# Two sums made by accumulating transfers from GpSimd's queue, and two more convolution steps in each round

## The chip, the cores and the metric

The kernel runs on one core of one Trainium2 chip. The metric is the device time of one execution in microseconds (us); lower is better. Each kernel is run several times, and medians are compared.

## The reference, cut to what matters

Two layers follow each other on 1024 latent tokens of width 1024. The first, an even layer, has two branches. Branch A gates and convolves over 31 tokens, normalises and gates again. Branch B runs a gated linear recurrence over the tokens in both directions and adds the two. One output projection takes both branches, and the result is added to the tokens `x`:

```python
va, vg, ga, xb, gb = jnp.split(h @ p["w_in"], ...)
y_a = conformer_conv(va, vg, p) * jax.nn.silu(ga)     # u = va*sigmoid(vg); conv; layernorm; silu
hs, hT = lru_scan(a, bx, h0, with_outputs)            # both directions
y_b = hs[:, :, 0] + hs[::-1, :, 1]                    # sum of the two directions
y_b = y_b * jax.nn.silu(gb)
out = jnp.concatenate([y_a, y_b], axis=-1) @ p["w_out"]
x = x + gate * out
```

The second layer, a pooling mixer, is not touched. Everything is fp32.

## The kernel before, in words

**Products.** Channels lie on the 128 partitions in 8 blocks (KT = 8), the 1024 tokens along the free axis in two halves of 512 (HALF, H = 512). An fp32 product is three matmuls on operands that are split into a high and a low part. For each weight of 128x1024, ScalarE casts the high part (`wh`) and GpSimd makes the low part (`wl = wr - wh`), in `raw_split`. PE uses `wl` in every third matmul, so it waits for GpSimd only there.

**The fixed order.** From the rounds to the end of the `ga` products, the helper `on` (line 670, which is why most rows carry L670) puts every instruction of an engine behind the one issued before it on that engine. So ScalarE, VectorE, GpSimd and PE do their work in the order in which the program is written: an instruction that waits holds back all that stand behind it. Transfers on SP's queue are placed by a scheduler.

**The rounds.** A loop over the 8 blocks j (L903) computes on PE `vg`, `va`, the gate matrices of the recurrence and `xb` of the next block. In round j, the recurrence of block j-1 (its state is `st`) goes on beside it: `rec_input` and the wide product on GpSimd, `rec_tanh` and `rec_exp` on ScalarE, and on VectorE `rec_scan`, two scans for each of the two directions. The tiles of a state, 128x1280 each (256 context and 1024 latent tokens), change their roles from round to round, so ScalarE writes a tile in the next round that was scanned in this one. At the round's end `rec_sum` adds the two directions on VectorE (128x1024) and SP stores the sum, 512 KB, to `yb_raw[j]` in DRAM. The residual of the next weight on GpSimd comes right behind. The 31-tap convolution of branch A is cut into steps on VectorE, one tap or pair of taps each. `fill(n)` puts n of these steps where it stands. A round ends with `fill(6)`; what is left of the convolutions is done behind the rounds.

**Behind the rounds.** The products `gb` 1 to 7 follow. `gated(n)` loads `yb_raw[n]` back in two halves (`yr`, L1223), multiplies it with `silu(gb)` (`sb`), splits it into `ybh` and `ybl`, and so forms the operand of the next product. That is `wob`, the second branch's share of the output projection: 8 blocks m of two halves. After each half `wob_evict` (L1254) scales PE's result on ScalarE into a tile `wo`, SP loads the half of the tokens `xT` into `xp`, GpSimd adds `wo` to it, and SP stores it to `x1_part` in DRAM (256 KB each). Much later `woa` (L1528) reads `x1_part` back and adds the first branch's share. Beside blocks 6 and 7 of `wob` runs the layer norm of branch A: squares on ScalarE into tiles `lsq`, sums on VectorE. Behind `wob` come the products `ga` of blocks 0 and 4.

**The ring of ScalarE's tiles.** `wo`, `lsq`, `sq_ln`, `mh`, `ml`, `sb` and others come from one pool, `tpool`, with four buffers (L60). A new tile can be written only when the last reader of the tile four places before it is done.

Of the kernel before, what the change touches and what calls it, by code (L numbers as in the profile page):

```python
# [17 lines left out]
C = 256  # L18
# [4 lines left out]
HALF = (slice(0, H), slice(H, S))  # L23
# [28 lines left out]
def body(ctx, tc, xT, ctxT, cc, ccol, modT, modW, win, gw, wout, wu, grp, wg, wo1, small, edge, ident, outT):  # L52
    nc = tc.nc
    mult, add, sub = ALU.mult, ALU.add, ALU.subtract
# [12 lines left out]
    yb_raw = [dram.tile([P, S], F32, tag=f"yb_raw{j}", name=f"yb_raw{j}") for j in range(KT)]  # L67
    y_raw = [{n: dram.tile([P, 2 * S], F32, tag=f"y_{n}_{p}", name=f"y_{n}_{p}") for n in BOPS} for p in range(2)]
    x1_part = [dram.tile([P, S], F32, tag=f"x1_part{j}", name=f"x1_part{j}") for j in range(KT)]
# [7 lines left out]
    def ttile(name):  # L77
        return tpool.tile([P, H], F32, tag="t", name=name)
# [22 lines left out]
    def held(after):  # L101
        return tc.issue_after(after.ins) if after is not None else nullcontext()
# [71 lines left out]
    def col(o, n=1):  # L174
        return sm[:, o : o + n]
# [121 lines left out]
    with ExitStack() as sctx:  # L297
# [36 lines left out]
        def cast(eng, n, part=slice(0, D)):  # L334
            hi = gs[n[1]][0] if isinstance(n, tuple) else w_tiles(n)[0]
            f = eng.copy if eng is A else lambda o, i: eng.tensor_copy(out=o, in_=i)
            f(hi[:, part], raws[n][:, part])
# [295 lines left out]
        for i in range(2):  # L633
            v = cx[i].rearrange("p (k n) -> p k n", n=C)
# [31 lines left out]
    def on(eng, f, *args, **kw):  # L666
        with ExitStack() as octx:
            if eng in last:
                octx.enter_context(tc.issue_after(last[eng].ins))
            last[eng] = f(*args, **kw)  # L670
        return last[eng]

    def act(*args, **kw):
        return on("act", nc.scalar.activation, *args, **kw)
# [4 lines left out]
    def gp(*args, **kw):  # L679
        return on("pool", nc.gpsimd.tensor_tensor, *args, **kw)  # L680
# [11 lines left out]
    def all_of(steps):  # L692
        for _ in steps:
            pass

    def raw_load(src, name):
        raw = wpool.tile([P, D], F32, tag="wr", name=f"wr_{name}")
        nc.sync.dma_start(raw, src)
        return raw
# [21 lines left out]
    def vec(f, **kw):  # L721
        return on("vec", f, **kw) if fixed[0] else f(**kw)
# [78 lines left out]
    def at_rest():  # L801
        ln_sums()
        while spread_[0] < min(whole_[0], ended[0] + 2, NSPREAD):
            spread_sum()
# [4 lines left out]
    def fill(n):  # L809
        while n > 0:  # L810
            try:
                next(going[0])
                n -= 1
            except StopIteration:
                if begun[0] >= whole_[0]:
                    return
                going[0] = conv(begun[0])
                begun[0] += 1

    with ExitStack() as actx:  # L820
# [42 lines left out]
        def rec_scan(st, d):  # L863
            at, iu = st[2][2 * d : 2 * d + 2]
            vec(nc.vector.scalar_tensor_tensor, out=iu, in0=at, scalar=1.0, in1=iu, op0=add, op1=mult)
            if d == 0:
                ctx_, lat = slice(0, C), slice(C, E)
                first = iu[:, C - 1 : C]
            else:
                ctx_, lat = slice(C - 1, None, -1), slice(E - 1, C - 1, -1)  # L870
                first = iu[:, 0:1]
            vec(nc.vector.tensor_tensor_scan, out=iu[:, ctx_], data0=at[:, ctx_], data1=iu[:, ctx_],
                initial=0.0, op0=mult, op1=add)
            vec(nc.vector.tensor_tensor_scan, out=iu[:, lat], data0=at[:, lat], data1=iu[:, lat],
                initial=first, op0=mult, op1=add)

        def rec_sum(st):
            hs, hb = st[2][1], st[2][3]
            vec(nc.vector.tensor_tensor, out=hs[:, C:], in0=hs[:, C:], in1=hb[:, C:], op=add)
            nc.sync.dma_start(yb_raw[st[0]], hs[:, C:])  # L880


        def gate_steps(j, w, u2, gates):
# [18 lines left out]
        state, free = None, [L[0], L[1], L[2], L[3], L[4], L[5]]  # L902
        for j in range(KT):  # L903
            final = j == KT - 1
# [65 lines left out]
            if state is None:  # L970
                for m in range(3 * KT - 2, 3 * KT):
                    gate_dot(m, gate_raw[m - 2 * KT])
                vec(nc.vector.tensor_tensor, out=m0[:, 0, 2 * KT :], in0=m0[:, 0, 2 * KT :],
                    in1=col(O_MB + 2 * KT, KT), op=add)
# [13 lines left out]
            if state is not None:  # L988
                for d in range(2):
                    rec_scan(state, d)  # L990
                rec_sum(state)
            at_rest()
            xb = wide(name if final else f"xb{j + 1}")
            steps = (x for h in range(2) for x in mm3_fixed(xb[:, HALF[h]], wnext, (hh, hl), HALF[h]))
# [12 lines left out]
                    w = raw_split(raw, name)  # L1007
                    rec_input(now, 0)
            all_of(steps)
            fill(19 if state is None else 6)  # L1010
            state, uc = now, ucn


# [38 lines left out]
        gb_product(3, gws[3])  # L1052
        fill(24)
        rec_scan(state, 0)
        raw = raw_load(win[4 * KT + 4], "gb4")
        hi = wpool.tile([P, D], F32R, tag="wh", name="wh_gb4")
        lo = wpool.tile([P, D], F32R, tag="wl", name="wl_gb4")
# [1 line left out]
        vec(nc.vector.tensor_tensor, out=lo, in0=raw, in1=hi.bitcast(F32), op=sub)  # L1059
        gws[4] = hi, lo  # L1060
        rec_scan(state, 1)
        rec_sum(state)
        at_rest()

    cpool.release()
# [4 lines left out]
    def d2tile(name, dt=F32):  # L1070
        return d2pool.tile([P, S], dt, tag="d2", name=name)
# [5 lines left out]
    def vtile(name):  # L1077
        return vpool.tile([P, H], F32, tag="v", name=name)
# [140 lines left out]
    def gated(n, between):  # L1219
        th, tl = d2tile(f"ybh{n}", F32R), d2tile(f"ybl{n}", F32R)  # L1220
        for h in range(2):
            y = vtile(f"yr{n}_{h}")
            nc.sync.dma_start(y, yb_raw[n][:, HALF[h]])  # L1223
            v = sbs[n][h]
            vec(nc.vector.tensor_tensor, out=v, in0=y, in1=v, op=mult)
            cast(th[:, HALF[h]], v)
            gp(out=tl[:, HALF[h]], in0=v, in1=th[:, HALF[h]].bitcast(F32), op=sub)
            fill(between)
        bh.append(th)
        bl.append(tl)  # L1230

    gb_product(4, gws[4])
    gated(0, 3)
    gb_silu(2)
    gb_weights(5)
    gb_product(5, gws[5])
    gated(1, 3)
    for j in range(3, KT + 1):
        if j == 4:
            gb_weights(j + 2)  # L1240
        if j < KT:
            gb_silu(j)
        if 4 < j < KT - 1:
            gb_weights(j + 2)
        if 3 < j < KT - 2:
            gb_product(j + 2, gws[j + 2])
        gated(j - 1, (0, 0, 4, 5, 5, 3, 1, 0)[j - 1])
        if j == KT:
            gb_weights(KT + 1)
            fill(8)  # L1250
        ln_sums()


    def wob_evict(m, h):  # L1254
        v = ttile(f"wo_{m}_{h}")
        act(v, wob_ps[m][h], AF.Identity, scale=m0[:, 0, 2 * KT + m : 2 * KT + m + 1])
        t = vtile(f"xp{m}_{h}")
        nc.sync.dma_start(t, xT[m][:, HALF[h]])
        gp(out=t, in0=t, in1=v, op=add)
        nc.sync.dma_start(x1_part[m][:, HALF[h]], t)  # L1260


    lnmu, lnsq = {}, {}
# [152 lines left out]
    for i in range(KH):  # L1416
        (b11, b12), (b21, b22) = [[us[j][:, h] for h in HALF] for j in (i, KH + i)]
        t1, t2, t3, t4 = b11, ttile(f"yat2_{i}"), b12, b21
        for j in (i, KH + i):
# [4 lines left out]
            for h in range(2):  # L1424
                if i:
# [3 lines left out]
                    v = us[j][:, HALF[h]]  # L1429
# [379 lines left out]
    for m in range(0, NK, 2):  # L1809
# [44 lines left out]
        elif m <= KT:  # L1854
            n = 2 * KT + m - 2
# [203 lines left out]
    def last_half0(m, w, ahead=None, pend=None):  # L2059
        p1, p2, p3, p4, p5, p6, p7 = w  # L2060
        a, d, b = psum(f"qa_l{m}"), psum(f"qd_l{m}"), psum(f"qb_l{m}")
        (x0, x1_), (y0, y1) = [[x1[m + i][:, h] for h in HALF] for i in range(2)]
        with held(linked_[0] if pend is not None else None):
            prod(a, p1, ops["b11"], True, False)
        with tc.high_priority(offset=EVAC):
            evac = nc.scalar.copy(b, a)
        if pend is None:
            mm = prod(d, p4, ops["t4"], True, True)
        else:
            mm = linked(d, p4, ops["t4"], True, True)  # L2070
        with tc.high_priority(offset=EVAC):
            gated(m + 1, y0, d)
        if pend is not None:
            pend("t4")
        nxt = None
        if ahead is not None:
            with tc.issue_after(evac.ins):
                nxt = ahead()
        with tc.issue_after(mm.ins):
            prod(b, p6, ops["t2"], False, False)  # L2080
        with tc.high_priority(offset=EVAC):
            gated(m, x1_, b)
        mm = prod(a, p2, ops["b21"], False, True)
        with tc.high_priority(offset=EVAC):
            gated(m, x0, a)
            fin_add(HALF[0], square(m, HALF[0]))
        with tc.issue_after(mm.ins):
            mm = prod(b, p7, ops["t3"], False, True)
        with tc.high_priority(offset=EVAC):
            gated(m + 1, y0, b)  # L2090
            fin_add(HALF[0], square(m + 1, HALF[0]))
            vec = gated(m + 1, y1, b)
        return nxt, mm, vec

    m = KT - 4
# [7 lines left out]
    wb, _, _ = last_half0(m, wa, last_weights, q2.run)  # L2103
# [230 lines left out]
```

## Time and profile before

| what | value |
|---|---|
| time, median of 3 runs | 1267.25 us (1265.35 to 1271.49) |
| span of the profiled execution | 1263.6 us |
| its own device time | not listed; only the span is |
| TensorE (PE) busy, granted clock | 1249.8 us (99%), 0.998 |
| VectorE (DVE) busy | 1139.3 us (90%) |
| ScalarE (ACT) busy | 653.8 us (52%) |
| GpSimd (POOL) busy | 295.7 us (23%) |

The span runs from the first to the last instruction on the core; the device time has a little around it. A row of the timeline has the start in us, the duration, the engine, the line, the operation with out<-in by the program's names, and in brackets the engine's idle time just before with the instruction or transfer that ended it. A row of the groups has the count, the busy time in us and the mean of one in ns. A row of the DMA issues has the size of one and the median time from issue to landing. A table by stretch has for each engine the busy time in it. The rounds last to about 412 us; the products `gb` to about 500, `wob` to about 586.

### The profile page before, as it was taken

The page shows a single profiled execution, that of the slowest core. Times are in us where ns is not written, and L with a number is a line of the kernel's source. Part 1 is how long each engine was busy: PE and PEld are TensorE (multiplying, and loading weights), DVE is VectorE, ACT ScalarE, POOL GpSimd, SP SyncE. Part 2 cuts the span into 40 slices and gives each one's busy share as a digit, 9 for nine tenths or more (in the row PEclk, how much of TensorE's full clock was granted, in tenths as well). Part 3 has the DMA queues.
Part 4 walks back from the last instruction along what each step waited for, and adds up shares of the span by engine and source line. Part 5 has one row for each costly group of instructions (what it writes and reads, how often), then busy time and mean ns, then how long its engine had stood idle before and what let it go on. Part 6 is the DMA issues. An engine that isn't in the chain of part 4 may idle for free.

```text
span 1263.6 us, 16209 instructions
## 1 busy us (share of the span) xinstructions
PE 1249.8 (99%) x5866; PEld 1035.6 (82%) x5866; DVE 1139.3 (90%) x1746; ACT 653.8 (52%) x952; POOL 295.7 (23%) x176
## 2 busy tenths in 40 slices
PE   9999999999999999999999999999999999999997
PEld 7788888888888888888887878888888888888786
DVE  7799999999999999998978969999899987977975
ACT  8464566656666534237535445744343444644642
POOL 0015364436444547543210023000000000000002
PEclk9999999999999999999999999999999999999999
DMA  9970121112121233442436666344323334759723
GB/s 376 388 254 33 52 65 46 63 43 75 42 84 42 84 119 132 159 150 84 147 112 225 202 206 183 103 136 148 125 94 140 117 125 126 268 199 335 285 71 134
DMA packets 78705, 182.29 MB, mean 144 GB/s; under 512 B 7712, under 2 KB 23328, under 8 KB 78624
## 3 DMA queue, kind: packets, MB, share of 16 engines
q1 hardware_dynamic: 67328, 172.33, 39.8%
q10 hardware_dynamic: 11296, 8.92, 2.2%
q8 instruction: 46, 0.75, 0.2%
q14 instruction: 35, 0.29, 0.1%
HBM read 137.18 MB, written 44.04 MB: 143 GB/s over the span
## 4 chain that ended last, share of the span: by engine, by line
PE 70%; DVE 18%; DMA 7%; issue 2%; ACT 2%; POOL 1%; SPq 0%; POOLq 0%; ACTq 0%; DVEq 0%
PE wob L670 7%; DVE conv L670 5%; PE va L670 5%; PE xb L670 4%; PE vg L670 4%; DVE l L670 3%; PE fold L670 3%; PE g L670 3%; PE qb_v L1153 2%; PE ga L670 2%; PE qb_g L1156 2%; PE ga L161 2%; PE qb_v L1156 2%; PE qb_g L1155 2%; PE qb_g L1153 2%
## 5 line engine op out<-in xcount | busy, mean ns | idle before, releaser
L670 DVE SCALAR_TENSOR_TENSOR conv<-u,sm,conv 128x505 f32<-128x505 f32 (+6 forms) x224 | 153.6, 744 | 1.0
L2045 POOL TENSOR_TENSOR o<-x,rr 128x256 f32<-128x256 f32 (+1 forms) x10 | 9.2, 952 | 448.4 <-ACT rr L2045 448.4
L670 ACT ACTIVATE l<-g,sm 128x512 f32<-128x512 f32 (+1 forms) x96 | 58.7, 619 | 57.7 <-PE g L670 57.0
L670 POOL TENSOR_TENSOR l<-l,l 128x1280 f32<-128x1280 f32 x16 | 47.1, 2967 | 25.6 <-ACT l L670 15.1
L670 PE MATMUL gb<-h0h,wl_gb 128*128 128x512 f32 x128 | 49.9, 390 | 0.4 <-POOL wl_gb L670 0.4
L670 PE MATMUL va<-h0h,wl_va 128*128 128x512 f32 x128 | 49.9, 390 | 0.2 <-DVE wl_va L670 0.2
L98 ACT CAST wq_g<-wr_g 128x512 fp32r<-128x512 f32 x48 | 28.2, 621 | 41.9 <-DMA wr_g<-wg 15.6
L670 PE MATMUL gb<-h0l,wh_gb 128*128 128x512 f32 x128 | 49.8, 389 | 0.0
L670 PE MATMUL gb<-h0h,wh_gb 128*128 128x512 f32 x128 | 49.8, 389 | 0.0
L670 PE MATMUL va<-h0l,wh_va 128*128 128x512 f32 x128 | 49.8, 389 | 0.0
L670 PE MATMUL va<-h0h,wh_va 128*128 128x512 f32 x128 | 49.8, 389 | 0.0
L670 PE MATMUL wob<-ybl,wh_wob 128*128 128x512 f32 x128 | 49.8, 389 | 0.0
L670 PE MATMUL wob<-ybh,wl_wob 128*128 128x512 f32 x128 | 49.8, 389 | 0.0
L670 PE MATMUL wob<-ybh,wh_wob 128*128 128x512 f32 x128 | 49.8, 389 | 0.0
L670 DVE TENSOR_TENSOR_SCAN l<-l,l 128x256 f32<-128x256 f32 (+1 forms) x32 | 48.7, 1521 | 1.1
L670 DVE SCALAR_TENSOR_TENSOR conv<-cL,wsum,conv 128x506 f32<-128x506 f32 (+3 forms) x70 | 48.1, 745 | 0.2
L670 POOL TENSOR_TENSOR l<-l,uc 128x1280 f32<-128x1280 f32 x16 | 47.6, 2999 | 0.0
L98 ACT CAST wq_wo<-wr_wo 128x512 fp32r<-128x512 f32 x48 | 28.6, 620 | 35.5 <-DVE wr_wo L1134 12.4
L98 ACT CAST wq_v<-wr_v 128x512 fp32r<-128x512 f32 x48 | 28.1, 620 | 33.7 <-DMA wr_v<-wfold 16.6
L670 PE MATMUL xb<-h0l,wh_xb 128*128 128x512 f32 x112 | 43.8, 391 | 0.0
L670 PE MATMUL xb<-h0h,wh_xb 128*128 128x512 f32 x112 | 43.8, 391 | 0.0
L670 POOL TENSOR_TENSOR wl_xb<-wr_xb,wh_xb 128x1024 fp32r<-128x1024 f32 x7 | 16.8, 2407 | 114.5 <-ACT wh_xb L670 114.5
(680 smaller groups left out, 4362.5 us busy)
## 6 DMA issues: line engine op xcount, KB each, us to landing
modw<-modW SPq DMA_DIRECT2D x16, 512.0 KB, 10.2
mod<-modT SPq DMA_DIRECT2D x32, 256.0 KB, 3.4
wr_v<-wfold SPq DMA_DIRECT2D x16, 512.0 KB, 4.0
wr_g<-wg SPq DMA_DIRECT2D x16, 512.0 KB, 4.3
wr_wo<-wo SPq DMA_DIRECT2D x16, 512.0 KB, 4.1
mod<-modT SPq DMA_DIRECT2D x14, 512.0 KB, 4.5
y_b<-y SPq DMA_DIRECT2D x24, 256.0 KB, 3.5
y_t<-y SPq DMA_DIRECT2D x24, 256.0 KB, 3.1
```

The lines of the kernel that those rows point to most:

```text
L98: return (nc.scalar.copy(hi, src), eng.tensor_tensor(out=lo, in0=src, in1=hi.bitcast(F32), op=sub))
L161: mm(ps, hi[:, kc], xh[k][:, cols], start=(k == 0), stop=False)
L670: last[eng] = f(*args, **kw)
L1153: nc.tensor.matmul(ps, hi, xh[k], start=(first and k == 0), stop=False, skip_group_check=not first)
L1155: nc.tensor.matmul(ps, hi, xl[k], start=False, stop=False, skip_group_check=not first)
L1156: mm = nc.tensor.matmul(ps, lo, xh[k], start=False, stop=(k == KH - 1), skip_group_check=not first)
L2045: tail[eng] = f(*args, **kw)
```

## The change

It has four parts. (1) `rec_sum` goes. `rec_store` stores the first direction plainly after its scan, on SP's queue, and after the second scan GpSimd issues a transfer that adds the second direction to it in DRAM (`accum_op=add`, 512 KB). (2) The rounds 1 to 6 end with `fill(8)` instead of `fill(6)`. (3) `gated(n)` issues, behind its second load, a copy of the tokens `xT[n]` to `x1_part[n]`, from DRAM to DRAM, 512 KB. (4) `wob_evict` no longer loads, adds and stores; GpSimd issues a transfer of the tile `wo` that adds it to `x1_part` (256 KB).

```diff
-        def rec_sum(st):
-            hs, hb = st[2][1], st[2][3]
-            vec(nc.vector.tensor_tensor, out=hs[:, C:], in0=hs[:, C:], in1=hb[:, C:], op=add)
-            nc.sync.dma_start(yb_raw[st[0]], hs[:, C:])
+        def rec_store(st, d):
+            latent = st[2][2 * d + 1][:, C:]
+            if d == 0:
+                nc.sync.dma_start(yb_raw[st[0]], latent)
+            else:
+                on("pool", nc.gpsimd.dma_start, yb_raw[st[0]], latent, accum_op=add)
...
                 for d in range(2):
                     rec_scan(state, d)
-                rec_sum(state)
+                    rec_store(state, d)
...
-            fill(19 if state is None else 6)
+            fill(19 if state is None else 6 if final else 8)
...
         rec_scan(state, 0)
+        rec_store(state, 0)
...
         rec_scan(state, 1)
-        rec_sum(state)
+        rec_store(state, 1)
...
-            nc.sync.dma_start(y, yb_raw[n][:, HALF[h]])
+            yl = nc.sync.dma_start(y, yb_raw[n][:, HALF[h]])
...
+        with held(yl):
+            nc.sync.dma_start(x1_part[n], xT[n])
...
-        t = vtile(f"xp{m}_{h}")
-        nc.sync.dma_start(t, xT[m][:, HALF[h]])
-        gp(out=t, in0=t, in1=v, op=add)
-        nc.sync.dma_start(x1_part[m][:, HALF[h]], t)
+        on("pool", nc.gpsimd.dma_start, x1_part[m][:, HALF[h]], v, accum_op=add)
```

`held(yl)` places the copy behind the load `yl` on the queue.

SP's queue behind the rounds, before (numbers behind names are buffers; `yb_raw_92` is that of block 7, `yb_raw_86` and `yb_raw_87` are those of blocks 1 and 2, `wr_gb_4108` is the weight of gb7, `cH` is used by another part):

```order
107 L880 DMA yb_raw_92<-l_914 128x1024
108 L1223 DMA yr_0_3976<-yb_raw_86 128x512
109 L256 DMA cH<-cc 128x512
110 L1223 DMA yr_1_3985<-yb_raw_86 128x512
111 L1223 DMA yr_0_3999<-yb_raw_87 128x512
112 L698 DMA wr_gb_4108<-win 128x1024
113 L1223 DMA yr_1_4008<-yb_raw_87 128x512
114 L1223 DMA yr_0_4079<-yb_raw_88 128x512
```

And in the changed kernel, where gb7's weight is `wr_gb_4124` and `x_part` is `x1_part`:

```order
107 L880 DMA yb_raw_92<-l_914 128x1024
108 L698 DMA wr_gb_4037<-win 128x1024
109 L1226 DMA yr_0_3990<-yb_raw_86 128x512
110 L1226 DMA yr_1_3998<-yb_raw_86 128x512
111 L1233 DMA x_part_108<-xT 16x8192
112 L256 DMA cH<-cc 128x512
113 L1226 DMA yr_0_4016<-yb_raw_87 128x512
114 L1226 DMA yr_1_4025<-yb_raw_87 128x512
115 L1233 DMA x_part_109<-xT 16x8192
116 L698 DMA wr_gb_4124<-win 128x1024
```

Both halves of a `yb_raw` tile are now loaded in a row, the second half of block 2's tile ahead of gb7's weight, and a copy of 512 KB stands behind each pair.

GpSimd in the last round and behind it, before (the names in brackets are the semaphores that an instruction waits for; `wl_gb` are the residuals for `gb`, `l` the tiles of the recurrence):

```order
90 L670 TENSOR_TENSOR l_909<-l_909,l_914 128x1280 [waits DVE_49,Activation_49,Pool_49]
91 L670 TENSOR_TENSOR wl_gb_3577<-wr_gb_3473,wh_gb_3576 128x1024 [waits PE_49,DMAHW3_49,Activation_49,Pool_49]
92 L670 TENSOR_TENSOR l_914<-l_914,uc_3168 128x1280 [waits DMAHW0_49,DVE_49,Pool_49]
96 L670 TENSOR_TENSOR l_913<-l_913,l_910 128x1280 [waits DVE_49,Activation_49,Pool_49]
97 L670 TENSOR_TENSOR wl_gb_3729<-wr_gb_3726,wh_gb_3728 128x1024 [waits DMAHW6_49,PE_49,Activation_49]
98 L670 TENSOR_TENSOR ybl_3895<-sb_0_3732,ybh_3894 128x512 [waits DMAHW2_49,Activation_49]
```

And in the changed kernel:

```order
96 L670 TENSOR_TENSOR l_909<-l_909,l_914 128x1280 [waits Activation_49,Pool_49]
97 L670 DMA yb_raw_91<-l_909 128x1024 [waits DMAHW6_49,DVE_49]
98 L670 TENSOR_TENSOR wl_gb_3594<-wr_gb_3488,wh_gb_3593 128x1024 [waits PE_49,DMAHW4_49,Activation_49,Pool_49]
99 L670 TENSOR_TENSOR l_914<-l_914,uc_3178 128x1280 [waits Pool_49]
104 L670 TENSOR_TENSOR wl_gb_3743<-wr_gb_3740,wh_gb_3742 128x1024 [waits DMAHW7_49,PE_49,Activation_49]
105 L670 DMA yb_raw_92<-l_913 128x1024 [waits DMAHW2_49,DVE_49]
106 L670 TENSOR_TENSOR ybl_3910<-sb_0_3746,ybh_3909 128x512 [waits DMASW7_49,Activation_49]
```

The accumulating transfer of block 6 stands between the last product of the recurrence and the residual for gb1, and waits for VectorE's scan. That of block 7 stands ahead of the first `ybl`, which now waits for a semaphore of GpSimd's own transfers (DMASW7).

ScalarE around the last half of `wob`, before (`wo_1` is the second half of block 7, `wh_ga` the high part of ga4's weight):

```order
405 L670 ACTIVATE wo_0_4920<-wob_0_4864,m_132 128x512 [waits Activation_49]
407 L670 ACTIVATE sq_ln_4954<-ms_ln_0_4950,eps_l 128x512 [waits DVE_49]
408 L670 CAST mh_ln_4956<-lnsum_902 128x512 [waits DVE_49]
409 L670 ACTIVATE wo_1_4960<-wob_1_4865,m_132 128x512 [waits Pool_49]
410 L670 CAST wh_ga_4968<-wr_ga_4966 128x1024 [waits DMAHW6_49]
```

And in the changed kernel:

```order
405 L670 ACTIVATE wo_0_4886<-wob_0_4830,m_132 128x512 [waits Activation_49]
407 L670 ACTIVATE sq_ln_4917<-ms_ln_0_4913,eps_l 128x512 [waits DVE_49]
408 L670 CAST mh_ln_4919<-lnsum_902 128x512 [waits DVE_49]
409 L670 ACTIVATE wo_1_4923<-wob_1_4831,m_132 128x512 [waits DMASW6_49,Activation_49]
410 L670 CAST wh_ga_4928<-wr_ga_4926 128x1024 [waits DMAHW4_49,Pool_49]
```

The instructions and their order are the same; `wo_1` waited for GpSimd's sum before, and waits now for the landing of a transfer.

## The prediction

> **What bounds the kernel now.** I read the page's busy times first, then the table by stretch for the region that the change touches, then TensorE's waits, and only then the timelines.
>
> ```profile
> PE 1249.8 (99%) x5866; PEld 1035.6 (82%) x5866; DVE 1139.3 (90%) x1746; ACT 653.8 (52%) x952; POOL 295.7 (23%) x176
> 200.00:410.00 210.00, 210.00 (x1000) 176.68 (x999) 203.92 (x259) 132.13 (x151) 101.79 (x40) 1.00 0.18 59
> 410.00:500.00 90.00, 89.55 (x396) 73.78 (x395) 86.61 (x121) 40.65 (x54) 53.09 (x28) 1.00 0.33 109
> 560.00:600.00 40.00, 40.00 (x177) 33.02 (x176) 35.79 (x48) 27.45 (x41) 12.76 (x8) 1.00 0.30 100
> core 0 of [0], span 1263.6 us
> ```
>
> In a stretch's row stand its length, then the busy time of PE, PEld, DVE, ACT and POOL. PE is busy for 1249.8 of 1263.6 us, at a granted clock of 1.00. It misses nothing of the 210 us of rounds, 0.45 us of the 90 behind them and nothing of the 40 at the end of the output product. VectorE, which the change relieves, is nearly as full (203.92 of 210), but it is not what the end waits for. So the question is not how much work is taken off VectorE. It is how much of PE's waiting can go, and how much the change puts in.
>
> ```profile
> PE fin_ms L2045 <- DVE dg L2045: 1.2, 1, 1.2
> PE qc_woa L1153 <- ACT wq_woa L98: 0.8, 1, 0.8
> PE gb L670 <- POOL wl_gb L670: 0.4, 1, 0.4
> ```
>
> These are PE's waits that matter here (total, times, longest). The first lies at the program's end, outside the change. The second, at 678 us, is behind it. Only the third lies inside.
>
> The profiled execution has no listed device time, only its span of 1263.6 us. The median of the runs shown is 1267.25, so 3.65 us lie around the span; I add that to every span below. About 0.5% (6.3 us) is what a measurement of this kernel can tell from no change.
>
> **The change part by part.**
>
> *Work taken off VectorE.*
>
> ```profile
> L670 DVE TENSOR_TENSOR l<-l,l 128x1024 f32<-128x1024 f32 x8 | 9.8, 1225 | 0.3
> 409.37 1.23 DVE L670 TENSOR_TENSOR l<-l,l 128x1024 f32<-128x1024 f32 x1
> 442.30 1.23 DVE L670 TENSOR_TENSOR l<-l,l 128x1024 f32<-128x1024 f32 x1
> L670 DVE SCALAR_TENSOR_TENSOR conv<-u,sm,conv 128x505 f32<-128x505 f32 x24 | 17.8, 742 | 0.2
> ```
>
> The eight sums of directions are 9.8 us. The 12 convolution steps (two in each of six rounds) only come earlier: 12 x 0.742 = 8.9 us that VectorE does not have to do later. In a round the exchange is nearly even, minus 1.23 plus 2 x 0.74, so 0.25 us more per round. After the rounds VectorE has up to 9 us in hand. PE did not wait for VectorE in these stretches, so the price of all this is 0, and the gain is 0 by itself. The cover for the extra 0.25 us is VectorE's own idle time in the rounds, 210 - 203.92 = 6.1 us; if it were gone, the extra would cost at most 6 x 0.25 = 1.5 us.
>
> *The wait that goes.* PE's 0.45 us at 479.89:
>
> ```profile
> 457.68 0.86 SPq L1223 DMA_DIRECT2D yr<-yb_raw  x2
> 461.78 1.47 DVE L670 TENSOR_TENSOR sb<-yr,sb 128x512 f32<-128x512 f32 x1 [1.37 <-DMA yr<-yb_raw]
> 476.24 3.59 POOL L670 TENSOR_TENSOR wl_gb<-wr_gb,wh_gb 128x1024 fp32r<-128x1024 f32 x1 [1.70 <-ACT wh_gb L670]
> 479.89 0.50 PE L670 MATMUL gb<-h0h,wl_gb 128*128 128x512 f32 x1 [0.45 <-POOL wl_gb L670]
> ```
>
> On SP's queue the second half of yb_raw's next tile stood behind the load of gb7's weight, which had to wait for a buffer. VectorE then stood 1.37 us for it, and everything up to the last weight residual shifted. In the changed order this load stands ahead of the weight, so at least 1.37 us come off a chain that was 0.45 us late: **-0.45 us**. The same queue now also takes eight copies xT to x1_part of 512 KB, each behind its yr loads; the next tile's loads stand behind a copy. That delays them by between 0 and one whole load of this kind (2.9 us, below); I take half, 1.5 us, covered by the 1.37 us won and VectorE's lead.
>
> *The accumulations of yb_raw.* GpSimd waits for scan 1 of VectorE, issues, and only then makes the next weight residual. Last round:
>
> ```profile
> 409.98 1.04 ACT L670 CAST wh_gb<-wr_gb 128x1024 fp32r<-128x1024 f32 x1
> 411.16 2.41 POOL L670 TENSOR_TENSOR wl_gb<-wr_gb,wh_gb 128x1024 fp32r<-128x1024 f32 x1 [11.48 <-DVE l L670]
> 413.97 0.39 PE L670 MATMUL gb<-h0h,wl_gb 128*128 128x512 f32 x1
> ```
>
> The scans end at 409.37 and the residual cannot start before the cast ends at 411.02. So GpSimd has 1.7 us for the issue, and 0.4 us more, since the residual ends at 413.57 and PE takes it at 413.97. Up to about 2 us of issue cost nothing. No row shows a DMA issued by GpSimd; on SP's queue an issue takes 0.43 us (0.86 for two). I take up to 2 us, cost **0**; at 3 us it would cost 1.
>
> At the end of the rounds the read of yb_raw waits for the last landing:
>
> ```profile
> 446.95 1.29 POOL L670 TENSOR_TENSOR ybl<-sb,ybh 128x512 fp32r<-128x512 f32 x1 [15.44 <-DMA yb_raw<-l]
> 451.35 1.78 POOL L670 TENSOR_TENSOR ybl<-sb,ybh 128x512 fp32r<-128x512 f32 x1 [3.11 <-ACT ybh L670]
> 454.82 2.41 POOL L670 TENSOR_TENSOR wl_gb<-wr_gb,wh_gb 128x1024 fp32r<-128x1024 f32 x1 [1.70 <-ACT wh_gb L670]
> ```
>
> The last scan ends at 442.30, so the accumulate starts there. GpSimd's first ybl would start at 442.3 plus the landing of 512 KB, against 446.95. Behind it on GpSimd stand idle times of 3.11 and 1.70 us before the residual that PE needs; I count the first. PE is reached when the landing takes over 446.95 + 3.1 - 442.3 = 7.8 us. A store of 512 KB takes 2.6, twice that is 5.2: cost **0**.
>
> *The output product.* Here sixteen loads, sixteen GpSimd sums (1.3 us each) and sixteen stores go, and sixteen accumulates of 256 KB come. They read the tile wo itself. That tile is one of a small ring on ScalarE, free before when GpSimd's sum had read it, and now only when the transfer has landed. Call L the time from GpSimd's turn to the landing.
>
> ```profile
> 562.41 1.30 POOL L670 TENSOR_TENSOR xp<-xp,wo 128x512 f32<-128x512 f32 x1 [1.95 <-issue]
> 565.59 0.63 ACT L670 ACTIVATE lsq<-u 128x512 f32<-128x512 f32 x1 [0.54 <-DVE u L670]
> 567.81 0.69 DVE L670 TENSOR_TENSOR mu<-mu,lsq 128x512 f32<-128x512 f32 x1
> 572.67 1.30 POOL L670 TENSOR_TENSOR xp<-xp,wo 128x512 f32<-128x512 f32 x1 [8.96 <-ACT wo L670]
> 577.52 0.70 DVE L670 TENSOR_TENSOR mu<-mu,lsq 128x512 f32<-128x512 f32 x1
> 583.43 1.29 POOL L670 TENSOR_TENSOR xp<-xp,wo 128x512 f32<-128x512 f32 x1 [7.09 <-issue]
> 585.70 0.69 ACT L670 ACTIVATE wo<-wob,m 128x512 f32<-128x512 f32 x1
> 586.28 1.04 ACT L670 CAST wh_ga<-wr_ga 128x1024 fp32r<-128x1024 f32 x1
> 587.72 2.40 POOL L670 TENSOR_TENSOR wl_ga<-wr_ga,wh_ga 128x1024 fp32r<-128x1024 f32 x1
> 590.70 0.40 PE L670 MATMUL ga<-h0h,wl_ga 128*128 128x512 f32 x1
> ```
>
> Three ScalarE instructions take a tile whose transfer is young. The square at 565.59 takes that of 562.41; VectorE uses its result at 567.81, so it may start at 567.18, and L up to 4.8 is free. A square behind takes that of 572.67; its sum stands at 577.52, so 576.89 will do: L up to 4.2, and 5.2 with 1 us of slack in what follows. The third is wo_7_1 at 585.70, which takes the tile of 583.43. Behind it in ScalarE's order is the cast wh_ga, behind that GpSimd's residual, behind that PE. From wo_7_1's start to the residual's end it is 0.58 (to the cast) + 1.04 + 2.40 + 0.14 of handover = 4.16 us. So the residual ends at 583.43 + L + 4.16 = 587.59 + L, and PE needs it at about 590.65. So the third wait costs PE L - 3.06 us. The first square's lateness, d = L - 4.8 (not under 0), shifts all that follows, and the second adds to it: before wo_7_0, ScalarE is L + d - 5.2 late (not under 0). **PE's wait is (L - 3.06) + (L + d - 5.2)**, each part not under 0. GpSimd's own issue stands between wo_7_1's end (0.69) and wl_ga, beside the cast: up to 0.58 + 1.04 - 0.69 = 0.93 us of it is hidden.
>
> L is the unknown:
>
> ```profile
> x_part<-xp SPq DMA_DIRECT2D x16, 256.0 KB, 2.0
> xp<-xT SPq DMA_DIRECT2D x16, 256.0 KB, 2.6
> yr<-yb_raw SPq DMA_DIRECT2D x16, 256.0 KB, 2.9
> yb_raw<-l SPq DMA_DIRECT2D x8, 512.0 KB, 2.6
> xp<-x_part SPq DMA_DIRECT2D x16, 256.0 KB, 6.1
> y_t4l<-y_t SPq DMA_DIRECT2D x2, 512.0 KB, 9.9
> ```
>
> These are median times from issue to landing. From below L is bounded by the plain store of the same bytes, 2.0; from above by the slowest row, 9.9. An accumulate reads the destination and writes it, so I take a store plus a load of that size, 2.0 + 2.6 = 4.6, near the two rows that do one half each. PE then waits 4.6 - 3.06 = **+1.5 us**. At L of 6.1 (the xp row) it would be 3.04 + 2.2 = 5.2.
>
> The Trainium skill, "DMA: Bandwidth & Descriptors", section "Anatomy of one DMA — SWDGE (gpsimd) path", gives for a transfer that GpSimd issues about 2.0 us plus the bytes at 436 GB/s. That would be an estimated 2.6 us for 256 KB and no wait at all. It says nothing there of the accumulation, and no row of this trace has one.
>
> *Sum.* -0.45 + 1.5 = +1.05. A PE that is late at 590 us loses some of its 0.8 us wait at 678 (ScalarE gains what PE lost); I count half, -0.4. So **+0.65 us**: span 1264.25, time 1267.9.
>
> **The rivals.**
> - *Landing like a plain load (L up to 3).* For it: the rows of 2.0 and 2.6. Against: read and write of the same bytes. No wait is added, -0.45: 1266.8; if the lead of VectorE also takes the 0.8 us at 678 and the 1.2 at the end, 1264.8. Chance 0.32. The figure of the Trainium skill above points the same way. Over 6.3 us faster would need more than the three waits of PE above together (2.4 us), hence 0.04 for that.
> - *Slower: the ring in series.* With L of 7, d is 2.2, the second part 7 + 2.2 - 5.2 = 4.0 and the third wait 3.94: 7.9 us, less the 0.85 won: +7.1, 1274.3. At 9.9 it is 6.84 + 9.8 = 16.6, so 1283. It decides from L = 6.75. For it: the rows of 6.1 and 9.9. Against: every row of the touched stretch (yr, xp from xT, x_part from xp, yb_raw) is at most 2.9, and the transfer engines' share from 560 to 600 us is 0.30. Chance 0.11.
> - *Issue is the cost.* If GpSimd needs 3.5 us per issue, the residual of the last round is 3.5 - 2 = 1.5 us late and wl_ga 3.5 - 0.93 = 2.6 more, besides the 1.5 for L: 5.6 less 0.85, +4.7, 1272.0. For it: nothing in the trace shows an issue by GpSimd. Against: GpSimd idles 7 to 9 us before most of its work (the rows at 572.67 and 583.43). Chance 0.12.
>
> ```profile
> L670 DVE TENSOR_SCALAR conv<-u,sm 128x512 f32<-128x512 f32 x16 | 11.2, 746 | 0.0
> ```
>
> The Trainium skill, "SBUF — State Buffer", section "Who interferes with whom", says that copies and tensor_scalar on VectorE can lock GpSimd out for the whole instruction, and that a DMA that GpSimd issues then waits for its descriptors; two-tensor sums do not do that. By it each scaling of the row above could stretch an issue by 0.75 us, two in a line by 1.5; beside the output product VectorE runs sums and one reciprocal. It keeps this rival's chance from being smaller; no row here shows such a wait.
> - *Nothing of it reaches PE or the wait of 0.45 stays:* 1267.25 to 1267.7, inside the forecast.
>
> **How the numbers follow.** The forecast (L between 3 and 6) has 0.45, the rivals 0.32, 0.11 and 0.12. The likeliest gives 1267.9. The forecast's own range is 1266.5 to 1271.5 (L of 3.06 to 6). With the fast case to 1264.0 and the slow ones to 1274.0 some 8 in 10 are inside. Slower by over 0.5% is over 1273.6: nearly all of the series rival and a little of the issue rival, 0.14 with the spread of the runs (1265.35 to 1271.49); faster by over 0.5%, under 1260.9, 0.04; the rest 0.82.
>
> **What would show it.** Right: the DMA rows give x_part from wo and yb_raw from the second direction about 4 to 5 us; wo_7_1 starts at about 588; PE's waits show one of 1 to 2 us at ga for wl_ga, and the one at gb for wl_gb is gone. VectorE's busy time is 9.8 us less and PE's the same. Wrong: a wait at wl_gb1 near 412 us (issue), a wait at ybl near 450 us that reaches PE (landing over 7.8 us), waits at wob for a yb tile (the copies are in the way), or waits of over 3 us at ga (L over 6).

## The result, and the profile after

The changed kernel takes 1277.52 us (median of 4 runs, 1276.94 to 1278.44), the kernel before 1267.56. The ratio is 1.0079 with a 95% interval of 1.0063 to 1.0095: slower by 10 us, where 1267.9 was forecast.

The page of the changed kernel, its busy times, and its table by stretch:

```profile
span 1276.3 us, 16180 instructions
PE 1255.1 (98%) x5866; PEld 1037.7 (81%) x5866; DVE 1132.9 (89%) x1738; ACT 653.3 (51%) x952; POOL 292.6 (23%) x184
...
200.00:410.00 210.00, 210.00 (x999) 176.69 (x999) 203.61 (x269) 132.22 (x150) 106.22 (x45) 1.00 0.26 74
440.00:460.00 20.00, 18.61 (x83) 15.07 (x81) 19.79 (x24) 2.85 (x5) 3.87 (x3) 1.00 0.57 155
460.00:480.00 20.00, 17.66 (x64) 14.00 (x65) 18.70 (x24) 8.54 (x15) 13.22 (x8) 0.83 0.55 195
```

VectorE has 6.4 us less to do, where 9.8 were forecast. The rounds are as full as before. The two executions that were profiled lie 12.7 us apart in span, more than the medians do: 1.4 us lie ahead of the `gb` products, 6.4 in them, 2.1 in the output product and at the start of `ga`, and about 3 far behind, from 1090 us on. So the largest part of the loss starts at 440 us: PE misses 3.7 us in 40, and from 460 to 480 us its granted clock is 0.83. PE's waits in the changed kernel say what it waited for:

```profile
PE gb L670 <- ACT wh_gb L670: 2.0, 1, 2.0
PE gb L670 <- POOL wl_gb L670: 1.8, 1, 1.8
...
PE ga L670 <- POOL wl_ga L670: 1.1, 1, 1.1
```

How much that is, the rows of the `gb` products show (count, shortest, median and longest in ns, from the first start to the last), first of the kernel before:

```profile
L670 PE MATMUL gb<-h0h,wh_gb x128: 389/389/397, 396.0 to 489.8; 128*128 128x512 f32 x128
```

And of the changed kernel:

```profile
L670 PE MATMUL gb<-h0h,wh_gb x128: 389/389/628, 397.4 to 497.6; 128*128 128x512 f32 x128
```

From the first to the last, the same matmuls take 100.2 instead of 93.8 us, 6.4 us more. Of that 3.7 are the two waits (less 0.45 before). The rest is the clock. PE in the changed kernel, around the two waits:

```profile
460.58 0.50 PE L670 MATMUL gb<-h0h,wh_gb 128*128 128x512 f32 x1 [1.97 <-ACT wh_gb L670]
...
463.07 0.79 PE L670 MATMUL gb<-h0h,wl_gb 128*128 128x512 f32 x1 [1.76 <-POOL wl_gb L670]
463.66 0.63 PE L670 MATMUL gb<-h0h,wh_gb 128*128 128x512 f32 x1
...
468.78 0.60 PE L670 MATMUL gb<-h0h,wh_gb 128*128 128x512 f32 x1
469.21 0.41 PE L670 MATMUL gb<-h0l,wh_gb 128*128 128x512 f32 x1
```

Between 463.66 and 468.78 us twelve matmuls start 0.427 us apart, where 0.227 is usual. Two waits that lie close (3.7 us idle within 4.5) cost almost as much again: 6.4 + 0.45 - 3.73 = 3.1 us. The Trainium skill, "TensorE: Matmul & The Clock Gate", section "Part 1: The HAM clock gate", has PE fall to half rate after an idle window of about 3.4 us. The spacing of 0.427 us here is such a half rate, but no single wait was longer than 2.0 us: two with a pair of matmuls between them were enough.

Now back from the waits to what was late. VectorE in the changed kernel, at the end of the 24 convolution steps ahead of the last scans:

```profile
411.20 15.68 DVE L670 SCALAR_TENSOR_TENSOR conv<-u,sm,conv 128x506 f32<-128x506 f32 x23
426.79 1.88 DVE L670 SCALAR_TENSOR_TENSOR edge_junk<-u,sm 128x8 f32<-128x8 f32 x1
428.72 3.40 DVE L670 TENSOR_TENSOR u<-u 128x512 f32<-128x512 f32 x1
433.13 1.80 DVE L670 SCALAR_TENSOR_TENSOR conv<-u,wsum 128x512 f32<-128x512 f32 x1
446.36 3.08 DVE L670 TENSOR_TENSOR_SCAN l<-l,l 128x256 f32<-128x256 f32 x2
```

The last scans and the same three instructions in the kernel before, where the three stand behind the scans:

```profile
439.19 3.08 DVE L670 TENSOR_TENSOR_SCAN l<-l,l 128x256 f32<-128x256 f32 x2
448.71 0.15 DVE L670 SCALAR_TENSOR_TENSOR edge_junk<-u,sm 128x8 f32<-128x8 f32 x1
448.90 0.69 DVE L670 TENSOR_TENSOR u<-u 128x512 f32<-128x512 f32 x1
450.61 0.76 DVE L670 SCALAR_TENSOR_TENSOR conv<-u,wsum 128x512 f32<-128x512 f32 x1
```

They are the boundary between the two parts of one block's convolution: an edge sum, the sum of the two halves of a tile, and the first tap on that sum. Each reads two operands from SBUF. Here they take 5.5 us more (1.73 + 2.71 + 1.04). The 23 steps ahead of them, whose running sum lies in PSUM, follow each other every 0.68 us (15.68 in all) as they do elsewhere, though GpSimd works beside most of them. GpSimd in the changed kernel shows what ran beside them, and what came of it:

```profile
425.69 5.88 POOL L670 TENSOR_TENSOR l<-l,l 128x1280 f32<-128x1280 f32 x2 [2.47 <-ACT l L670]
431.51 2.87 POOL L670 TENSOR_TENSOR wl_gb<-wr_gb,wh_gb 128x1024 fp32r<-128x1024 f32 x1
449.74 0.88 POOL L670 DMA_DIRECT2D yb_raw<-l  x1 [15.36 <-DVE l L670]
455.97 2.99 POOL L670 TENSOR_TENSOR ybl<-sb,ybh 128x512 fp32r<-128x512 f32 x2 [5.35 <-DMA yb_raw<-l]
460.66 2.36 POOL L670 TENSOR_TENSOR wl_gb<-wr_gb,wh_gb 128x1024 fp32r<-128x1024 f32 x1 [1.70 <-issue]
```

Each ends within its usual length after the GpSimd instruction that ran beside it: the edge sum at 428.67 and the first wide product at about 428.6 (half of the row's 5.88 us), the sum of halves at 432.12 and the second product at 431.57, the tap at 434.93 and the residual at 434.38. So the last scan ends at 449.44 instead of 442.27, or 5.8 us late when the 1.4 us are taken off by which this execution's rounds began later. The accumulation lands, the first `ybl` starts at 455.97 instead of 446.95, and behind it stand the cast and the residual of the next weight.

In the output product the prediction's wait is there. ScalarE, GpSimd and PE of the changed kernel:

```profile
591.92 0.88 POOL L670 DMA_DIRECT2D x_part<-wo  x1 [7.45 <-ACT wo L670]
596.04 0.69 ACT L670 ACTIVATE wo<-wob,m 128x512 f32<-128x512 f32 x1 [1.92 <-DMA x_part<-wo]
597.75 2.55 POOL L670 TENSOR_TENSOR wl_ga<-wr_ga,wh_ga 128x1024 fp32r<-128x1024 f32 x1
600.36 0.50 PE L670 MATMUL ga<-h0h,wl_ga 128*128 128x512 f32 x1 [1.08 <-POOL wl_ga L670]
```

And its DMA issues, with the median time to landing:

```profile
yb_raw<-l SPq DMA_DIRECT2D x8, 512.0 KB, 2.6
yb_raw<-l POOLq DMA_DIRECT2D x8, 512.0 KB, 5.0
x_part<-wo POOLq DMA_DIRECT2D x16, 256.0 KB, 4.0
```

### The profile page after: what moved, and what is told of

It reads as the page before. It is cut to its first block, busy times and chain, and to the rows that moved or that the text cites. A ratio compares the mean times of both kernels' runs of the same rounds, so it can differ in the third digit from the quotient of the medians.

```text
span 1276.3 us, 16180 instructions
## 1 busy us (share of the span) xinstructions
PE 1255.1 (98%) x5866; PEld 1037.7 (81%) x5866; DVE 1132.9 (89%) x1738; ACT 653.3 (51%) x952; POOL 292.6 (23%) x184
## 5 line engine op out<-in xcount | busy, mean ns | idle before, releaser
L670 PE MATMUL vg<-h0l,wh_vg 128*128 128x512 f32 x112 | 43.6, 389 | 0.0
L670 PE MATMUL xb<-h0h,wl_xb 128*128 128x512 f32 x112 | 43.6, 389 | 0.0
```

## The experiments

Theory A: the two steps more per round move a block's boundary beside GpSimd's wide products, where three of its instructions are held up, and all that hangs on the last scans comes late. Rival B: the accumulating transfers make the loss by themselves.

**Six steps per round again.**

```diff
-            fill(19 if state is None else 6 if final else 8)
+            fill(19 if state is None else 6)
```

> The changed kernel, with the rounds 1 to 6 ending with 6 convolution steps again (both kinds of accumulating transfers stay). Theory A: the earlier steps put a block's boundary (edge sum, sum of the two halves, first pair tap) beside GpSimd's two wide products of the last state, where three VectorE instructions took 1.8 + 3.4 + 1.8 us instead of 0.15 + 0.7 + 0.75; without it the last scan ends near 443.7 us instead of 449.4, the first ybl starts near 450 instead of 456.0, PE's two waits at gb (2.0 and 1.8 us) fall to under 0.6 together, the clock stays at 1.00 between 460 and 470 us, and the time is about 1271. Rival B: the accumulating transfers alone (landing 5.0 us for 512 KB, GpSimd's waits) make the loss: the waits at gb stay over 2 us together and the time stays over 1275.

1271.31 us, ratio 1.0027 (1.0017 to 1.0038), so 6.2 us (0.5%) of the 10 are gone. Its waits of PE at gb:

```profile
PE gb L670 <- POOL wl_gb L670: 1.2, 2, 0.7
```

And its stretches from 450 us on:

```profile
450.00:460.00 10.00, 9.30 (x42) 7.38 (x41) 9.93 (x14) 3.65 (x7) 5.61 (x4) 1.00 0.42 134
460.00:470.00 10.00, 10.00 (x46) 8.29 (x45) 8.29 (x11) 4.88 (x8) 6.22 (x5) 1.00 0.64 229
```

The clock stays at 1.00. The waits at gb are 1.2 us, more than the 0.6 expected, so not all of the loss is in the steps.

**The steps alone, on the kernel before.**

```diff
-            fill(19 if state is None else 6)
+            fill(19 if state is None else 6 if final else 8)
```

> The kernel before, with the two convolution steps more in rounds 1 to 6 and nothing else of the change. Theory A: the same three VectorE instructions are stretched beside GpSimd's products, the last scan ends about 5 us later than before, the sum and its store follow, PE waits 1 to 4 us at gb and the time is 1270 to 1274. Rival B: no accumulating transfer, so no loss: 1267.5 give or take 1.

1273.07 us, ratio 1.0037 (1.0023 to 1.0052). There is no transfer from GpSimd in this kernel, and two of the three instructions are held up all the same (the third starts after the residual has ended, and is not):

```profile
427.05 2.47 DVE L670 SCALAR_TENSOR_TENSOR edge_junk<-u,sm 128x8 f32<-128x8 f32 x1
429.57 2.83 DVE L670 TENSOR_TENSOR u<-u 128x512 f32<-128x512 f32 x1
433.42 0.76 DVE L670 SCALAR_TENSOR_TENSOR conv<-u,wsum 128x512 f32<-128x512 f32 x1
```

PE waits 1.6 and 1.8 us at gb, and its clock falls here too (0.79 from 460 to 465 us, 0.87 to 470). Rival B as the whole cause falls: about half of the loss comes without any of the change's transfers.

**The wide products left out.** GpSimd's two products of the last state are dropped (the scaling of the recurrence's input in block 7 is left out); the rest is the changed kernel.

```diff
         rec_root(state)
-        for d in range(2):
-            rec_scaled(state, d)
         gb_weights(3)
```

> The changed kernel without GpSimd's two wide products of the last block's state (the scaling of the recurrence's input in block 7 is left out), everything else in place. Lock theory: the edge sum and the sum of the two halves, both with two operands in SBUF, wait for GpSimd's two products of 2.9 us each; without these products they take 0.15 and 0.7 us instead of 1.9 and 3.4, the last scan ends about 4 to 6 us earlier and PE's waits at gb are under 1 us together. Rival: these instructions are long at that place by themselves (their operands were written just before, or the conv bank is the cause): they stay at 1.8 us or more and 2.8 us or more.

One execution, 1271.92 us. VectorE in it:

```profile
425.30 0.16 DVE L670 SCALAR_TENSOR_TENSOR edge_junk<-u,sm 128x8 f32<-128x8 f32 x1
425.50 0.69 DVE L670 TENSOR_TENSOR u<-u 128x512 f32<-128x512 f32 x1
427.21 2.48 DVE L670 SCALAR_TENSOR_TENSOR conv<-u,wsum 128x512 f32<-128x512 f32 x1
441.12 3.08 DVE L670 TENSOR_TENSOR_SCAN l<-l,l 128x256 f32<-128x256 f32 x2
```

And GpSimd:

```profile
426.74 2.39 POOL L670 TENSOR_TENSOR wl_gb<-wr_gb,wh_gb 128x1024 fp32r<-128x1024 f32 x1 [5.01 <-ACT wh_gb L670]
```

The first two have their usual length at the same place in the program. The third, which now meets the residual (426.74 to 429.13), is held to 429.69. It is the GpSimd instruction beside them that makes these instructions long: without it two are short, and with another one the third is long. The last scan ends at 444.20, 3.7 us sooner than in the changed kernel when the 1.5 us are taken off by which these rounds began sooner. That is what the three instructions save, 5.5 less the 1.7 that the third still loses. PE's waits at gb are 1.0 us.

**The boundary behind the scans.** The other way to get it out of GpSimd's way, with wo in the other ring (below).

```diff
-        fill(24)
+        fill(15)
         rec_scan(state, 0)
...
         at_rest()
+        fill(9)
```

> The changed kernel, eight steps per round kept, with wo in the other ring and with the 24 steps ahead of the last scans cut to 15; the other 9, which hold the block's boundary, stand behind the scans. Theory A: the boundary no longer meets GpSimd's wide products, the scans may start as soon as these products are done; the last scan ends near 441 us or earlier, no wait at gb over 0.5 us, clock 1.00; the time is 1266 to 1269, as the kernel before or better by up to 1 us. Rival B (accumulating transfers are the loss): 1271 or more. A third possibility: the scans themselves have two operands in SBUF and are stretched beside GpSimd's products; then the scan's end gains less than the 9 steps' 6 us.

1275.03 us, ratio 1.0061 (1.0042 to 1.0080): the third possibility. VectorE:

```profile
428.08 4.22 DVE L670 SCALAR_TENSOR_TENSOR l<-l,l 128x1280 f32<-128x1280 f32 x1 [2.21 <-POOL l L670]
432.33 5.15 DVE L670 TENSOR_TENSOR_SCAN l<-l,l 128x256 f32<-128x256 f32 x2
...
443.03 0.14 DVE L670 SCALAR_TENSOR_TENSOR edge_junk<-u,sm 128x8 f32<-128x8 f32 x1
```

And its GpSimd and ScalarE behind the scans:

```profile
430.90 3.65 POOL L670 TENSOR_TENSOR wl_gb<-wr_gb,wh_gb 128x1024 fp32r<-128x1024 f32 x1
```

```profile
452.60 0.63 ACT L257 ACTIVATE cH<-cH 128x512 f32<-128x512 f32 x1 [15.86 <-DMA cH<-cc]
```

The edge sum is short again, but now the scan's first instruction takes 4.22 instead of 1.48 us and the first pair of scans 5.15 instead of 3.08, and GpSimd's residual 3.65 instead of 2.41: both sides lose. The scans end at 443.1, 5.3 us sooner than in the changed kernel when the later start of its rounds is taken off. Yet the 9 steps stand behind them, and ScalarE's casts for `ybl` stand behind a load of `cH` that landed late, so `ybl` starts only at 453.83.

**The sum on VectorE again, in the changed kernel.**

```diff
         def rec_store(st, d):
-            latent = st[2][2 * d + 1][:, C:]
-            if d == 0:
-                nc.sync.dma_start(yb_raw[st[0]], latent)
-            else:
-                on("pool", nc.gpsimd.dma_start, yb_raw[st[0]], latent, accum_op=add)
+            hs, hb = st[2][1], st[2][3]
+            if d == 1:
+                vec(nc.vector.tensor_tensor, out=hs[:, C:], in0=hs[:, C:], in1=hb[:, C:], op=add)
+                nc.sync.dma_start(yb_raw[st[0]], hs[:, C:])
```

> The changed kernel with the sum of the two directions on VectorE and a plain store again; the two more steps and the accumulation of the tokens stay. Theory A: the scans end late as in the changed kernel, the store lands in 2.6 instead of 5.0 us but the sum takes 1.2, so PE still waits about 1 to 3 us at gb: 1273 to 1276. Rival B: the loss at gb goes wholly, about 1271.

1276.45 us, ratio 1.0072 (1.0053 to 1.0091); PE still waits 2.4 and 1.8 us at gb. With the scans late, these runs show no difference between the two ways of making the sum (the intervals overlap).

**wo in its own ring.**

```diff
-        v = ttile(f"wo_{m}_{h}")
+        v = vtile(f"wo_{m}_{h}")
```

> The changed kernel with the tiles wo taken from the ring of yr and xp (free at that time) instead of the ring of ScalarE's tiles, so that squares and later wo do not wait for the landing of a 256 KB accumulation. If the wait of 1.1 us at ga for wl_ga is the ring's (landing of 4.0 us, worked out in the prediction as L - 3.06), it goes and the time is 1.0 to 1.5 us less, 1276 to 1276.5. If it comes from GpSimd's issue or from the loads in the queue, it stays and the time is that of the changed kernel.

1275.66 us, ratio 1.0062 (1.0047 to 1.0077): 1.9 us less by the medians, with an interval that overlaps the changed kernel's; in the trace PE has no wait at ga. The wait was the ring's.

**Plain transfers in the output product** (the addition of the tokens is left out).

```diff
-        on("pool", nc.gpsimd.dma_start, x1_part[m][:, HALF[h]], v, accum_op=add)
+        on("pool", nc.gpsimd.dma_start, x1_part[m][:, HALF[h]], v)
```

> The changed kernel with plain transfers from GpSimd's queue in wob_evict instead of accumulating ones (the addition of the tokens is left out; same bytes, same queue, same waits). If the reading of the destination makes the landing long: about 2.6 us instead of 4.0, wo_7_1 starts 1.4 us earlier and the wait at ga (1.1) goes to under 0.3. If the queue of GpSimd makes it: 3.5 to 4.0 and the wait at ga stays about 1.

Its DMA issues in that place:

```profile
x_part<-wo POOLq DMA_DIRECT2D x16, 256.0 KB, 2.3
```

2.3 us to landing instead of 4.0, and no wait at ga. The time, 1276.64 us (ratio 1.0071, 1.0056 to 1.0086), shows little of it, 0.9 us by the medians, within the intervals; in the profiled execution the waits at gb (3.2 and 1.8 us) were longer than in the changed kernel's.

**Six steps and its own ring.** Both edits above together.

> The changed kernel with six steps per round again and wo in the other ring: only the transfers' cost in the products gb is left. Theory A: the wait at ga (1.1 us) goes and with it about 1 to 2 us against the kernel with six steps alone (1271.3 measured): 1269 to 1270.5, so 1 to 3 us above before. Rival (the ring isn't the cause at ga): 1271.

1270.08 us, ratio 1.0018 (1.0008 to 1.0027); no wait at ga. **The third and fourth parts alone**, with the own ring, the sum on VectorE and six steps (the three edits of these names together):

> The change's third and fourth parts alone (copies of the tokens, accumulation of the output product), with wo in the other ring; the sum of directions on VectorE with a plain store and six steps per round as before. If what is left of the loss in the kernel with six steps and its own ring (1270.1) comes from the accumulation of yb_raw, this one is at the kernel before, 1266.5 to 1268. If it comes from the copies or from GpSimd's issues in the output product, it stays near 1270.

1267.87 us, ratio 1.0002 (0.9991 to 1.0014), no different from before; PE waits 0.5 us at gb and 0.6 at wob. **The first part alone**, on the kernel before (of the change's diff only the lines with `rec_sum` and `rec_store`):

> The change's first part alone: plain store of the first direction, accumulation of the second, nothing else. ScalarE's write into the accumulated tile waits for the landing (5.0 us), so GpSimd's wide products come about 1.2 us later and the last scans meet the residual behind them: waits at gb about 1.0 instead of 0.45 us, time 1268 to 1270. If the first part costs nothing (as forecast): 1266.5 to 1267.8.

1269.79 us, ratio 1.0019 (1.0008 to 1.0030). In its ScalarE row tanh waits for the landing in the last round, and in its VectorE row the last scans run into the residual:

```profile
415.05 2.62 ACT L670 ACTIVATE l<-l,chalf 128x1280 f32<-128x1280 f32 x2 [1.15 <-DMA yb_raw<-l]
```

```profile
432.64 5.15 DVE L670 TENSOR_TENSOR_SCAN l<-l,l 128x256 f32<-128x256 f32 x2
```

PE waits 0.9 us at gb. **The first part with a plain transfer** from GpSimd (the sum of the directions is left out):

```diff
-                on("pool", nc.gpsimd.dma_start, yb_raw[st[0]], latent, accum_op=add)
+                on("pool", nc.gpsimd.dma_start, yb_raw[st[0]], latent)
```

> The kernel with the first part alone, with a plain transfer from GpSimd's queue for the second direction instead of an accumulating one (the sum of the two directions is left out; same bytes, same queue, same waits). If the first part's loss (0.19% measured, 2.4 us) comes from the long landing of the accumulation (5.0 to 5.5 us for 512 KB), the landing falls to about 3 us, ScalarE's tanh no longer waits for it, the scans are no longer stretched, PE's waits at gb go to 0.5 us and the time is 1267.0 to 1268.2. If the loss comes from GpSimd's place in the chain or from the order of the queues, the time stays at 1269 to 1270.

The row of its transfers for the second direction:

```profile
yb_raw<-l POOLq DMA_DIRECT2D x8, 512.0 KB, 3.0
```

The landing takes 3.0 us, ScalarE no longer waits, PE waits nowhere at gb. But the time is 1269.20 us (ratio 1.0013, 1.0002 to 1.0025), only 0.6 us less, with an interval that overlaps the other's. So the wait of ScalarE is the long landing's, and the waits at gb go with it (one trace each), but that the landing costs the time is not shown. The trace of this kernel can't say where the rest lies: its execution took 1266.78 us, 2.4 under the median.

**The kernel before, once more**, for a second profile:

> The kernel before once more, for a second profile of it: its first one has PE's stretch from the first to the last qc_wo matmul at 75.7 us, where the changed kernels show 76 to 80 with waits for wq_wo. If these waits belong to the runs and not to the change, they show here too (0.5 us or more); else none does.

One execution, 1267.59 us, span 1265.8: no wait for wq_wo; its `qc_wo` matmuls take 75.8 us, against 76.0 to 79.9 in the changed kernels. It waits 0.6 us at gb and 0.7 us at wob, where the first profile has 0.4 and none, so waits of that size come and go between executions of one kernel.

## Why the prediction was wrong

**The step that failed** is "the price of all this is 0, and the gain is 0 by itself" for the work taken off VectorE. It priced a convolution step by its mean of 0.742 us, and "VectorE has up to 9 us in hand" after the rounds, and set 1.5 us as the most that the extra work in the rounds could cost. The steps are not alike: those at a block's boundary read two operands from SBUF and are held up beside GpSimd. Counting 12 steps moved did not ask which steps then stand beside which GpSimd instruction. Moved, they made the last scans 5.8 us late. By the ratios the steps are worth 0.0079 - 0.0027 = 0.0052, 6.6 us, in the changed kernel, and 4.7 us on the kernel before.

**The rule was at hand.** The Trainium skill, "SBUF — State Buffer", section "Who interferes with whom", was drawn on in the prediction only for GpSimd's issue. The same section says that a VectorE instruction with two SBUF inputs contends with a GpSimd instruction that reads SBUF; the traces here agree, in both directions, with 0.15 us grown to 1.9 and 2.41 to 3.65. Beside the issues themselves no hold was seen: an accumulating issue took 0.88 us.

**The landing of yb_raw.** The bound of 7.8 us was counted from a scan's end at 442.30. The landing itself, about 6 us from the issue at 449.74 to the first `ybl`, was under the bound; it was the start that moved. Also unforeseen: with six steps PE waits 0.7 us at gb near 458 us, where it did not wait before. There ScalarE's tanh waits 1.4 us for the landing in the last round (0.9 to 1.4 in the kernels with this accumulation), so GpSimd's wide products come later and the first scans meet the residual (5.16 instead of 3.08 us). The prediction did not price this.

**The 0.45 us at 479.89** were to go, since SP loads the second half ahead of gb7's weight. They did not: where PE reaches this place in time, a wait of 0.5 us is still there with the loads in the new order (with six steps, with the own ring besides, and with the output product's parts alone). In the changed kernel, where PE comes later, none is there.

**The output product: right.** "A store plus a load" gave L = 4.6; measured 4.0 in the middle, and 596.04 - 591.92 = 4.12 at the place that counts. The formula L - 3.06 gives 1.06 us; PE waited 1.08. That it fits to 0.02 is luck: the chain from wo_7_1 to the residual's end took 4.26 us where 4.16 was counted, and PE needed the residual 0.14 us later after the issue than counted. The ring was its cause (own ring: no wait). The second square's ring wait (1.18 us on ScalarE, for the transfer issued at 581.16) reached nobody, as worked out for an L up to 4.2. A plain transfer from GpSimd takes 2.3 us, near the 2.6 that the prediction estimated by the Trainium skill, "DMA: Bandwidth & Descriptors", section "Anatomy of one DMA — SWDGE (gpsimd) path"; the accumulation adds the rest.

**The 0.4 us counted back at 678 us** did not come. That wait is 0.8 us in every other kernel profiled, however late PE was, and 1.5 in the changed one.

**The issue: right.** Of the 2 us held free in the last round 0.88 are used (410.40 to 411.28), and no wait is at gb1.

**The clock** was not in the sum at all. It added 3.1 us to two waits that were 3.7 together.

**What stays open.** By the ratios the sum is 6.6 us for the steps, 1.1 for the ring (0.0027 - 0.0018), 2.0 for the accumulation of yb_raw (0.0018 - 0.0002) and 0.3 for the rest, 10 together. Only the first is clear of the noise; the intervals behind the others overlap. Of the 2.0, the waits at gb are about 0.5. The rest was not located: the executions that were profiled show waits at other places far behind (wq_wo). Each of the twelve altered kernels has them (0.2 to 1.9 us), also the one with the steps alone, which has none of these transfers, and neither profile of the kernel before has. Why, no run shows.

## What to carry to other kernels

A step that is moved must be looked at by its operands, not by its mean: with two operands in SBUF it can cost what is left of the GpSimd instruction that it meets, and GpSimd can lose too. An accumulating transfer keeps its source 1.7 times as long as a plain one of the same bytes (4.0 against 2.3 us, 5.0 against 3.0), so the ring of its source and the next writer of its tile belong in the sum. Work taken off an engine that nobody waits for gained nothing here, and its reordering cost more than all else.

## What the runs showed of the hardware

- Two waits of PE of 2.0 and 1.8 us with two matmuls between them brought the granted clock to half: 0.427 instead of 0.227 us per matmul for twelve matmuls. Waits of 1.6 and 1.8 us (the steps alone) did it too, for some seven matmuls. With 1.0 and 1.8 us (the boundary behind the scans) the clock stayed at 1.00.
- Landing of GpSimd's transfers: 256 KB accumulating 4.0 to 4.2 us, plain 2.3; 512 KB accumulating 5.0 to 5.4, plain 3.0. Issue on GpSimd 0.85 to 0.89 us accumulating; plain 0.54 to 0.56 for 256 KB and 0.59 to 0.60 for 512.
- VectorE beside a GpSimd instruction that reads SBUF: a scan's first product 4.22 instead of 1.48 us, a pair of scans 5.15 instead of 3.08, an edge sum of 8 elements up to 2.47 instead of 0.15. Convolution steps with one operand in PSUM kept their 0.68 us.
